# Gate and up projections with the tokens as the stationary operand, in parts of 14 and 8 column groups

## The chip, the cores and the metric

The kernel runs on one core of a Trainium2 chip. The metric is the device time of one execution in microseconds. TensorE (PE, with its weight loads as PEld), VectorE (DVE), ScalarE (ACT), GpSimd (POOL) and SyncE (SP, which issues the transfers) run side by side and wait for one another by semaphores. A matmul has a stationary operand, loaded first, and a moving one, whose columns stream through; its result lands in PSUM, which has eight banks of 512 float32 columns.

## What is computed

One layer of an encoder for 256 tokens of width 2048, conditioned by one vector c: a feed-forward, a mixer (a gated branch and latent attention side by side), a second feed-forward, and norms. Cut to what the change touches:

```
mod = silu(c) @ w_ada + b_ada                 # 9 rows of 2048: shift, scale, gate three times
n = rms(h, norm) * (1 + scale) + shift        # 256 x 2048
a = silu(n @ w_gate) * (n @ w_up)             # 256 x 5632
h = h + 0.5 * gate * (a @ w_down)             # 256 x 2048
```

All weights are float32 and are read from memory once: 2048 x 5632 for each of gate, up and down, in both feed-forwards.

## The kernel before

The activations are kept transposed, with the features on the partitions: h and n are 16 row blocks of 128 features by 256 tokens. Every matrix product is made of three: each weight block is split into a high part, rounded to the engine's fast float32 form, and a low part, the rest (`split`: one transfer into one of five raw buffers, a cast on ScalarE, line 170, and a subtraction on VectorE, line 174, for each of two halves; there are four buffers for high and four for low halves, two blocks' worth). The activations are split in the same way. High by high, high by low and low by high are added up in PSUM.

A feed-forward (`ffn`) works on 22 column groups (`pg`) of 128 x 2 gate and 128 x 2 up columns, in two halves of 11. A half first makes the products of all its groups, then its share of the down projection, so 22 slots of activations `a` (128 features x 256 tokens, high and low part, pool `actp`) are alive at a time. In `gu_chunk` a 128 x 128 weight block is stationary and the 256 tokens move:

```python
mm(o, hi[:, k, f], n[0][:, kt], first and kt == kt0 and f % 2 == 0, False)
mm(o, hi[:, k, f], n[1][:, kt], False, False)
```

so gate and up of 128 features stand side by side in one bank, features on the partitions, and `swiglu` (tanh on ScalarE, three operations on VectorE and a cast on ScalarE) turns a bank into a slot of the form that the down projection moves.

The modulation rows are made column by column: `mod_col` loads a 128 x 2048 block of w_ada (1 MB) into one of the raw buffers, and VectorE multiplies it by silu(c) and sums along the row (line 132, tile ada). There are 144 of these. Feed-forward 1 can't wait for its own: its first half goes over the 16 row blocks in groups of 3, 3, 3, 3 and 4 (`grouped`), so that each group starts when its rows are there; between groups the partial sums are copied from PSUM to SBUF (`keep_part`, line 288) and later back (`take_part`, line 292). The first three row blocks go through four column groups at once, in all eight banks. Feed-forward 2 does the same in three passes (`in_passes`). The other columns are spread over later work by lists of counts: `ADA_UP1` for the second half's up projection, `ADA_DOWN1` for the down projections and `ADA_MIX` for the mixer; `ada` pins each product behind the last subtraction of the block before it on VectorE.

The mixer's projections already hold the tokens stationary (`a_form`), 128 at a time, and move up to 512 weight columns.

The tile framework sets the order on each engine: it goes through the program with costs of its own and issues on an engine what is ready, in program order where several are. `issue_after` pins an instruction behind another one. On the chip each engine then keeps that order, waits included.

Of the kernel before, what the change touches and what calls it, by code (L numbers as in the profile page):

```python
# [2 lines left out]

# [13 lines left out]
P = 128  # L17
# [5 lines left out]
HALF_PG = 11  # L23
FK = 22
# [3 lines left out]
ADA_UP1 = (0, 2, 4, 4, 1, 1, 4, 2, 2, 2, 4)  # L28
ADA_DOWN1 = (1, 1, 1, 1, 2, 1, 0, 0, 1, 2, 2, 0, 1, 0, 1, 1)
# [3 lines left out]
    "outA": (0, 1, 1, 2, 0, 0, 0, 0), "outM": (1, 1, 0, 1, 1, 0, 0, 0),  # L33
# [37 lines left out]
def encoder_layer(ctx: ExitStack, tc: tile.TileContext, xT, pos, cst, vnorm, w_ada, gu1k, gu1, dn1,  # L71
                  win_a, win_b, wuq, wukv, w_sT, wout, gu2, dn2, outT, *gu1g):
# [50 lines left out]
    # ---- conditioning: one column of the modulation table per 128 x 2048 block of w_ada  # L123
# [38 lines left out]
    # ---- weights: exact high and low parts  # L162
# [15 lines left out]
    # ---- norms  # L178
# [6 lines left out]
    class RowNorm:  # L185
        """Root mean square over the partitions and tiles of a transposed array."""
# [57 lines left out]
    # ---- feed-forward  # L244
    def acc_of(banks, f):
        return banks[f // 2][:, (f % 2) * T : (f % 2) * T + T]

    def gu_chunk(w, banks, n, kt0, nk, first, last):
        kts = [range(kt0, kt0 + (nk + 1) // 2), range(kt0 + (nk + 1) // 2, kt0 + nk)]
        for (whi, wlo), ks in zip(w, kts):  # L250
            hi, lo = (x.rearrange("p (k f c) -> p k f c", k=len(ks), f=4) for x in (whi, wlo))
            for k, kt in enumerate(ks):
                for f in range(4):
                    o = acc_of(banks, f)
                    mm(o, hi[:, k, f], n[0][:, kt], first and kt == kt0 and f % 2 == 0, False)
                    mm(o, hi[:, k, f], n[1][:, kt], False, False)
            for k, kt in enumerate(ks):
                for f in range(4):
                    mm(acc_of(banks, f), lo[:, k, f], n[0][:, kt], False, last and kt == kt0 + nk - 1)

    def swiglu(ftmp, src, slot):
        g, u = src[:, :T], src[:, T:]
        th = ftmp.tile([P, T], F32, tag="th", name="th")
        s = ftmp.tile([P, T], F32, tag="sg", name="sg")
        a = ftmp.tile([P, T], F32, tag="a", name="a")
        act.activation(th, g, AF.Tanh, scale=0.5)
        dve.scalar_tensor_tensor(s, th, 1.0, g, op0=ALU.add, op1=ALU.mult)
        dve.tensor_tensor(a, s, u, op=ALU.mult)
        act.copy(slot[:, 0], a)  # L269
        dve.tensor_tensor(slot[:, 1], a, slot[:, 0].bitcast(F32), op=ALU.subtract)  # L270

    def ffn(gu, dn, n, gate, ada_pg, ada_dn, lead, groups, prep, norm, before_down=None):
        with tc.tile_pool(name="actp", bufs=1) as actp, tc.tile_pool(name="ftmp", bufs=2) as ftmp:
            def tag(pg):
                return "acc" if pg % 2 == 0 else "aux"

            def finish(pg, banks, slots):
                for j in range(2):
                    f = pg * 2 + j
                    slot = actp.tile([P, 2, T], F32R, tag=f"a{f % FK}", name=f"s{f}")  # L280
                    swiglu(ftmp, banks[j], slot)
                    slots.append(slot)

            def keep_part(part, pg, banks):
                for j in range(2):
                    f = pg * 2 + j
                    part[f] = actp.tile([P, 512], F32, tag=f"a{f % FK}", name=f"p{f}")
                    act.copy(part[f], banks[j])  # L288

            def take_part(part, pg, banks):  # L290
                for j in range(2):
                    act.copy(banks[j], part[pg * 2 + j])  # L292

            def in_passes(slots):
                part = {}
                for kgs in PASSES:
                    for pg in range(HALF_PG):
                        banks = [bank(tag(pg), "gu") for _ in range(2)]
                        for kg in kgs:
                            prep(kg, pg)  # L300
                            w = split(gu[pg, kg])
                            if kg and kg == kgs[0]:
                                take_part(part, pg, banks)
                            gu_chunk(w, banks, n, kg * 4, 4, kg == 0, kg == 3)
                        if kgs[-1] == 3:
                            finish(pg, banks, slots)
                        else:
                            keep_part(part, pg, banks)

            def grouped(slots):  # L310
                part = {}

                banks = [bank(tag(pg), "gu") for pg in range(4) for _ in range(2)]
                for kt in range(GROUPS[0]):
# [3 lines left out]
                    for half in range(2):  # L318
                        hi, lo = (x.rearrange("p (f c) -> p f c", f=8) for x in w[half])
                        for f in range(8):  # L320
                            o = acc_of(banks, half * 8 + f)
                            mm(o, hi[:, f], n[0][:, kt], kt == 0 and f % 2 == 0, False)
                            mm(o, hi[:, f], n[1][:, kt], False, False)
                        for f in range(8):
                            mm(acc_of(banks, half * 8 + f), lo[:, f], n[0][:, kt], False, kt == GROUPS[0] - 1)
                todo = []
# [7 lines left out]
                def load(kg, kt0, pg, a, b):  # L334
                    if a == 0:
                        prep(kg, pg)
                    return split(groups[kg][pg][:, a * 512 : b * 512], (b - a) * 512, (b - a + 1) // 2 * 512)

                w = load(*todo[0])
                for pg in range(4):  # L340
                    keep_part(part, pg, banks[2 * pg : 2 * pg + 2])
                for i, (kg, kt0, pg, a, b) in enumerate(todo):
                    if a == 0:
                        banks = [bank(tag(pg), "gu") for _ in range(2)]
                        if kg:
                            take_part(part, pg, banks)
                    gu_chunk(w, banks, n, kt0 + a, b - a, kg == 0 and a == 0, b == GROUPS[kg])
                    if i + 1 < len(todo):
                        w = load(*todo[i + 1])
                    if b == GROUPS[kg]:  # L350
                        if kg < len(GROUPS) - 1:
                            keep_part(part, pg, banks)
                        else:
                            finish(pg, banks, slots)

            for half in range(2):
                pgs = range(half * HALF_PG, half * HALF_PG + HALF_PG)
                slots = []
                if half == 0:
                    (grouped if lead is not None else in_passes)(slots)  # L360
                else:
                    for i, pg in enumerate(pgs):
                        banks = [bank(tag(pg), "gu") for _ in range(2)]
                        for kg in range(4):
                            w = split(gu[pg - (HALF_PG if lead is not None else 0), kg])
                            if kg < ada_pg[half][i]:
                                ada(1)
                            gu_chunk(w, banks, n, kg * 4, 4, kg == 0, kg == 3)
                        finish(pg, banks, slots)
                for d in range(KT):  # L370
# [3 lines left out]
                    for c2 in range(2):  # L374
                        w = split(dn[half, d, c2], 11 * P, 6 * P)
                        if c2 < ada_dn[half][d]:
                            ada(1)
# [13 lines left out]
    # ---- silu(c) * 2 on every partition  # L391
# [55 lines left out]
    # ---- feed-forward 1  # L447
# [11 lines left out]
    for kg, nk in enumerate(GROUPS[:-1]):  # L459
        at += nk  # L460
        pgs = range(4 if kg == 0 else 0, HALF_PG)
# [28 lines left out]

    ffn(gu1, dn1, n1, G1, (none, ADA_UP1), (none, ADA_DOWN1), gu1k, gu1g, prep1, norm, gate_col(G1))
# [68 lines left out]
        # low-rank queries  # L560
# [12 lines left out]
        # low-rank keys and values, shared rotary key  # L573
# [430 lines left out]
```

## Time and profile before

| | us |
|---|---|
| three runs | 1870.49, 1872.46, 1872.83 |
| median | 1872.46 |
| profiled execution: span from first to last instruction | 1868.8 |
| busy in the span: TensorE | 1834.1 |
| weight loads | 1795.9 |
| VectorE | 1324.0 |
| ScalarE | 970.1 |

The profiled execution is known by its span; what lies around the span is taken from the median of the runs, 3.7 us above it. The stages on TensorE begin at about 20 (feed-forward 1), 800 (mixer) and 1095 us (feed-forward 2).

### The profile page before, as it was taken

Reading aid. Unit: us, or ns where it says so; the run is one execution under the profiler, and the core shown is the slowest. Engines: PE = TensorE matmul, PEld = TensorE weight load, DVE = VectorE, ACT = ScalarE, POOL = GpSimd, SP = SyncE. Lnnn points to the kernel's source line nnn. Section 1 sums busy time; section 2 is a strip of 40 time slices with the busy share of each in tenths; the row PEclk is TensorE's granted clock in tenths of the full one; section 3 lists DMA queues with packets and bytes.
Section 4 is the critical chain, followed back from the end, with each engine's and each line's share of the span. In section 5 each row is a group of like instructions: output and inputs, shape, how many; then the busy total and the mean of one; then the engine's idle time right before and its main releaser. Section 6 shows DMA issues by size and latency. Waiting matters only on the chain.

```text
span 1868.8 us, 34895 instructions
## 1 busy us (share of the span) xinstructions
PE 1834.1 (98%) x14512; PEld 1795.9 (96%) x14512; DVE 1324.0 (71%) x1849; ACT 970.1 (52%) x1553; POOL 30.2 (2%) x29
## 2 busy tenths in 40 slices
PE   6999999999999999999999999999999999999997
PEld 6999999999999999988878999999999999999997
DVE  6888878776867687796877876666887655554554
ACT  3688874344444444466674554567634344443553
POOL 1000000000000000000010000000000000000000
PEclk7999999999999999999999999999999999999998
DMA  8989958997968788877855667776599755554552
GB/s 329 332 322 337 343 177 284 318 321 257 358 235 317 274 304 297 327 266 280 311 185 198 229 221 272 273 276 234 175 317 318 278 181 183 186 187 148 173 184 92
DMA packets 75326, 481.22 MB, mean 257 GB/s; under 512 B 8480, under 2 KB 9248, under 8 KB 33184
## 3 DMA queue, kind: packets, MB, share of 16 engines
q1 hardware_dynamic: 75168, 479.00, 71.7%
q8 instruction: 113, 1.85, 0.4%
q14 instruction: 45, 0.37, 0.1%
HBM read 476.87 MB, written 2.10 MB: 256 GB/s over the span
## 4 chain that ended last, share of the span: by engine, by line
PE 55%; issue 41%; DVE 2%; ACT 1%; DMA 0%; POOL 0%; DVEq 0%; SPq 0%; ACTq 0%; POOLq 0%
PE gu L121 27%; PE dn L121 14%; PE wo L121 5%; PE u L121 2%; PE v L121 2%; PE cq L121 1%; PE sc L121 1%; DVE ada L132 1%; PE ckv L121 1%; PE qproj L121 1%; PE av L121 0%; ACT whi L170 0%; DMA h<-in_xT_dram 0%; PE vproj L121 0%; PE kproj L121 0%
## 5 line engine op out<-in xcount | busy, mean ns | idle before, releaser
L174 DVE TENSOR_TENSOR wlo<-raw,whi 128x1024 fp32r<-128x1024 f32 (+3 forms) x717 | 760.7, 1067 | 425.1 <-ACT whi L170 409.2
L170 ACT CAST whi<-raw 128x1024 fp32r<-128x1024 f32 (+2 forms) x720 | 663.2, 925 | 738.4 <-PE gu L121 404.8
L121 PE MATMUL gu<-nh,whi 128*128 128x256 f32 x2816 | 695.1, 284 | 11.5 <-ACT whi L170 11.3
L121 PE MATMUL gu<-nl,whi 128*128 128x256 f32 x2816 | 694.4, 284 | 0.0
L121 PEld LDWEIGHTS gu<-nh,whi 128*128 128x128 f32 x2816 | 542.7, 193 | 12.9 <-ACT whi L170 12.5
L121 PEld LDWEIGHTS gu<-nl,whi 128*128 128x128 f32 x2816 | 542.7, 193 | 0.2 <-DVE nl L242 0.2
L121 PE MATMUL gu<-nh,wlo 128*128 128x256 f32 x2816 | 400.8, 284 | 0.0
L121 PE MATMUL dn<-s,whi 128*128 128x256 f32 x2816 | 379.6, 283 | 0.0
L121 PEld LDWEIGHTS gu<-nh,wlo 128*128 128x128 f32 x2816 | 367.1, 193 | 0.0
L121 PEld LDWEIGHTS dn<-s,whi 128*128 128x128 f32 x2816 | 356.4, 192 | 0.0
L132 DVE CUSTOM_DVE_ANT_0 ada<-ada,cb 128x2048 f32<-128x2048 f32 (+1 forms) x144 | 324.5, 2255 | 0.0
L121 PE MATMUL dn<-s,wlo 128*128 128x256 f32 x1408 | 210.7, 283 | 0.0
L121 PEld LDWEIGHTS dn<-s,wlo 128*128 128x128 f32 x1408 | 187.4, 192 | 0.0
L288 ACT COPY p<-gu 128x512 f32<-128x512 f32 x132 | 70.7, 589 | 27.3 <-PE gu L121 26.9
L292 ACT COPY gu<-p 128x512 f32<-128x512 f32 x132 | 74.3, 597 | 0.0
L387 DVE SCALAR_TENSOR_TENSOR h<-dn,mods,h 128x256 f32<-128x256 f32 x64 | 30.9, 483 | 39.4 <-PE dn L121 39.4
L241 ACT ACTIVATE nh<-nr,mods 128x256 fp32r<-128x256 f32 x48 | 23.2, 507 | 41.8 <-DVE mods L143 34.2
L121 PE MATMUL wo<-mA,whi 128*128 128x256 f32 x256 | 35.8, 288 | 0.0
L197 ACT ACTIVATE sq<-h 128x256 f32<-128x256 f32 x45 | 18.8, 418 | 30.0 <-DVE h L387 19.8
L270 DVE TENSOR_TENSOR s<-a,s 128x256 fp32r<-128x256 f32 x88 | 33.2, 418 | 0.5 <-ACT s L269 0.5
L242 DVE SCALAR_TENSOR_TENSOR nl<-nr,mods,nh 128x256 fp32r<-128x256 f32 x48 | 22.2, 481 | 15.9 <-ACT nh L241 15.8
L121 PE MATMUL wo<-mM,whi 128*128 128x256 f32 x256 | 33.3, 283 | 0.0
(206 smaller groups left out, 1045.7 us busy)
## 6 DMA issues: line engine op xcount, KB each, us to landing
ada<-in_w_ada_dram SPq DMA_DIRECT2D x144, 1024.0 KB, 6.6
raw<-in_gu_dram SPq DMA_DIRECT2D x143, 1024.0 KB, 5.1
raw<-in_dn_dram SPq DMA_DIRECT2D x128, 704.0 KB, 5.3
raw<-in_gu_dram SPq DMA_DIRECT2D x40, 768.0 KB, 6.2
raw<-in_win_a_dram SPq DMA_DIRECT2D x20, 1024.0 KB, 6.6
raw<-in_wout_dram SPq DMA_DIRECT2D x16, 1024.0 KB, 5.1
raw<-in_gu1k_dram SPq DMA_DIRECT2D x3, 1024.0 KB, 8.8
raw<-in_wuq_dram SPq DMA_DIRECT2D x4, 768.0 KB, 5.0
```

The source lines that it names most:

```text
L121: return pe.matmul(out, w, x, start=start, stop=stop, skip_group_check=True)
L132: dve.tensor_tensor_reduce(out=w[:, sl], in0=w[:, sl], in1=cb[:, sl], scale=0.5, scalar=acc if i else 0.0, op0=ALU.mult, op1=ALU.add, accu ...
L170: mark["act"] = act.copy(hi, raw[:, a:b])
L174: mark["dve"] = dve.tensor_tensor(lo, raw[:, a:b], hi.bitcast(F32), op=ALU.subtract)
L197: act.activation(sq, src, AF.Square)
L241: act.activation(hi, nr, AF.Identity, bias=s)
L242: dve.scalar_tensor_tensor(lo, nr, s, hi.bitcast(F32), op0=ALU.add, op1=ALU.subtract)
L270: dve.tensor_tensor(slot[:, 1], a, slot[:, 0].bitcast(F32), op=ALU.subtract)
L288: act.copy(part[f], banks[j])
L292: act.copy(banks[j], part[pg * 2 + j])
L387: dve.scalar_tensor_tensor(h[:, d], o, mods[:, gate, d : d + 1], h[:, d], op0=ALU.mult, op1=ALU.add)
```

## The change

Gate and up now take 128 tokens as the stationary operand and move 512 columns: for each row block of a column group, two gate and two up blocks side by side, once for each half of the tokens. The products come out with tokens on the partitions. `finish` makes the swiglu in that form, and a `flip`, queued behind the matmuls of the next step, transposes the group's 256 features by four matmuls with the identity into a PSUM bank, from which ScalarE casts the high part and VectorE subtracts the low part of two slots at once. The halves become parts of 14 and 8 groups (`FIRST`), and with them the down projections: two blocks of 14 slots for each output row block in the first, one of 16 in the second. `run` holds a common loop for all steps; it puts the partial sums of the next step into its banks right behind the matmuls of this one, before this step's sums are kept. The counts in the `ADA` lists are new. The weights are laid out to match on the host. Comments were dropped.

```diff
-HALF_PG = 11
-FK = 22
+FIRST = 14
 GROUPS = (3, 3, 3, 3, 4)
 PASSES = ((0, 1), (2,), (3,))
 EARLY = 4 * len(PASSES[0])
-ADA_UP1 = (0, 2, 4, 4, 1, 1, 4, 2, 2, 2, 4)
-ADA_DOWN1 = (1, 1, 1, 1, 2, 1, 0, 0, 1, 2, 2, 0, 1, 0, 1, 1)
+ADA_UP1 = (2, 3, 2, 3, 2, 3, 2, 3)
+ADA_DOWN1 = ((0, 0, 0, 1) * 4, (1, 1, 1, 1, 1, 1, 1, 1, 1, 1, 1, 1, 1, 1, 0, 0))
 ADA_MIX = {
     "ckv": (2, 1, 0, 1), "v0": (0, 1, 0, 1), "v1": (1, 0, 0, 0),
     "u0": (1, 2, 0, 2), "u1": (1, 1, 1, 0),
-    "outA": (0, 1, 1, 2, 0, 0, 0, 0), "outM": (1, 1, 0, 1, 1, 0, 0, 0),
+    "outA": (0, 1, 1, 2, 0, 0, 0, 0), "outM": (1, 1, 1, 1, 1, 1, 1, 0),
 }
...
             for k, kt in enumerate(ks):
-                for f in range(4):
-                    o = acc_of(banks, f)
-                    mm(o, hi[:, k, f], n[0][:, kt], first and kt == kt0 and f % 2 == 0, False)
-                    mm(o, hi[:, k, f], n[1][:, kt], False, False)
+                for t in range(2):
+                    mm(banks[t], n[0][:, kt, token(t)], hi[:, k], first and kt == kt0, False)
+                    mm(banks[t], n[1][:, kt, token(t)], hi[:, k], False, False)
             for k, kt in enumerate(ks):
-                for f in range(4):
-                    mm(acc_of(banks, f), lo[:, k, f], n[0][:, kt], False, last and kt == kt0 + nk - 1)
-
-    def swiglu(ftmp, src, slot):
+                for t in range(2):
+                    mark["gu"] = mm(banks[t], n[0][:, kt, token(t)], lo[:, k], False, last and kt == kt0 + nk - 1)
...
-        act.copy(slot[:, 0], a)
-        dve.tensor_tensor(slot[:, 1], a, slot[:, 0].bitcast(F32), op=ALU.subtract)
+        return a
...
+            flips = []
+
             def finish(pg, banks, slots):
-                for j in range(2):
-                    f = pg * 2 + j
-                    slot = actp.tile([P, 2, T], F32R, tag=f"a{f % FK}", name=f"s{f}")
-                    swiglu(ftmp, banks[j], slot)
-                    slots.append(slot)
+
+                a = [swiglu(ftmp, banks[t]) for t in range(2)]
+                slot = actp.tile([P, 2, 2, T], F32R, tag=f"a{pg % FIRST}", name=f"s{pg}")
+                slots += [(slot[:, 0, j], slot[:, 1, j]) for j in range(2)]
+
+                def flip():
+                    ps = bank(tag(pg), "tps")
+                    with tc.issue_after(mark["gu"].ins):
+                        for j in range(2):
+                            for t in range(2):
+                                o = j * T + t * P
+                                pe.matmul(ps[:, o : o + P], a[t][:, j * P : j * P + P], ident, start=o == 0, stop=True,
+                                          is_transpose=True, skip_group_check=True)
+                    hi, lo = (slot[:, i].rearrange("p a b -> p (a b)") for i in range(2))
+                    act.copy(hi, ps)
+                    dve.tensor_tensor(lo, ps, hi.bitcast(F32), op=ALU.subtract)
+
+                flips.append(flip)
+
+            def turn(n=1):
+                for _ in range(min(n, len(flips))):
+                    flips.pop(0)()
...
             def take_part(part, pg, banks):
-                for j in range(2):
-                    act.copy(banks[j], part[pg * 2 + j])
+                for t in range(2):
+                    act.copy(banks[t], part[pg][:, t])
+
+            def run(steps, part, slots):
+
+
+                def begin(pg, kt0, nk, opens, load, more):
+                    w = load()
+                    if not opens:
+                        return w, banks
+                    new = [bank(tag(pg), "gu") for _ in range(2)]
+                    if kt0:
+                        take_part(part, pg, new)
+                    return w, new
+
+                banks = None
+                w, banks = begin(*steps[0])
+                for i, (pg, kt0, nk, opens, load, more) in enumerate(steps):
+                    gu_chunk(w, banks, n, kt0, nk, kt0 == 0, kt0 + nk == KT)
+                    if not opens or nk == 4:
+                        turn()
+                    old = banks
+                    if i + 1 < len(steps):
+                        w, banks = begin(*steps[i + 1])
+                    if kt0 + nk == KT:
+                        finish(pg, old, slots)
+                    elif not more:
+                        keep_part(part, pg, old)
...
-                    for pg in range(0 if kg else 4, HALF_PG):
-                        todo += [(kg, kt0, pg, a, b) for a, b in zip(cuts, cuts[1:])]
+                    for pg in range(0 if kg else 4, FIRST):
+                        steps += [(pg, kt0 + a, b - a, a == 0, partial(load, kg, pg, a, b), b < nk)
+                                  for a, b in zip(cuts, cuts[1:])]
...
+            def rest(slots):
+                def load(pg, kg):
+                    w = split(gu[pg - (FIRST if lead is not None else 0), kg])
+                    if kg < ada_pg[pg - FIRST]:
+                        ada(1)
+                    return w
+
+                run([(pg, kg * 4, 4, kg == 0, partial(load, pg, kg), kg < 3)
+                     for pg in range(FIRST, NPG) for kg in range(4)], {}, slots)
...
+                chunks, size = ((2, FIRST), (1, 2 * (NPG - FIRST)))[half]
+                cut = (size + 1) // 2
                 for d in range(KT):
                     if half == 0 and before_down:
                         before_down(d)
                     o = bank("acc" if d % 2 else "aux", "dn")[:, :T]
-                    for c2 in range(2):
-                        w = split(dn[half, d, c2], 11 * P, 6 * P)
-                        if c2 < ada_dn[half][d]:
-                            ada(1)
-                        for part_, k0 in ((0, 0), (1, 6)):
+                    for c2 in range(chunks):
+                        w = split(dn[half][d, c2], size * P, cut * P)
+                        if not c2:
+                            ada(ada_dn[half][d])
+                        for part_, (k0, k1) in enumerate(((0, cut), (cut, size))):
                             hi, lo = (x.rearrange("p (k c) -> p k c", c=P) for x in w[part_])
-                            ks = range(6 if part_ == 0 else 5)
-                            for k in ks:
-                                a = slots[c2 * 11 + k0 + k]
-                                mm(o, hi[:, k], a[:, 0], c2 == 0 and part_ == 0 and k == 0, False)
-                                mm(o, hi[:, k], a[:, 1], False, False)
-                            for k in ks:
-                                mm(o, lo[:, k], slots[c2 * 11 + k0 + k][:, 0], False, c2 == 1 and k0 + k == 10)
+                            if part_:
+                                turn()
+                            for k in range(k0, k1):
+                                a = slots[c2 * size + k]
+                                mm(o, hi[:, k - k0], a[0], c2 == 0 and k == 0, False)
+                                mm(o, hi[:, k - k0], a[1], False, False)
+                            for k in range(k0, k1):
+                                mark["gu"] = mm(o, lo[:, k - k0], slots[c2 * size + k][0], False,
+                                                c2 == chunks - 1 and k == size - 1)
                     dve.scalar_tensor_tensor(h[:, d], o, mods[:, gate, d : d + 1], h[:, d], op0=ALU.mult, op1=ALU.add)
```

## Rows read from the trace of the kernel before

**Rows 1.** The page: busy time by engine, and granted clock over 40 slices.

```profile
span 1868.8 us, 34895 instructions
...
PE 1834.1 (98%) x14512; PEld 1795.9 (96%) x14512; DVE 1324.0 (71%) x1849; ACT 970.1 (52%) x1553; POOL 30.2 (2%) x29
...
PEclk7999999999999999999999999999999999999998
```

**Rows 2.** The chain of waits: start us, us, engine, tile, line, count.

```profile
42.27 28.88 PE gu L121 x226
...
72.76 4.35 PE gu L121 x34
...
79.11 210.50 PE gu L121 x1752
289.61 126.72 PE dn L121 x1056
416.33 253.44 PE gu L121 x2112
...
822.87 14.07 PE ckv L121 x96
836.94 0.87 PE tp L540 x8
...
849.40 21.77 PE v L121 x96
...
972.55 0.44 PE tpp L806 x4
...
993.02 0.59 PE tpp L806 x4
```

**Rows 3.** The page: groups, with busy us, mean ns, idle before.

```profile
L121 PE MATMUL gu<-nh,whi 128*128 128x256 f32 x2816 | 695.1, 284 | 11.5 <-ACT whi L170 11.3
...
L292 ACT COPY gu<-p 128x512 f32<-128x512 f32 x132 | 74.3, 597 | 0.0
```

**Rows 4.** Windows: stretch, its us, busy by engine (instructions), clock, DMA share, GB/s.

```profile
120.00:160.00 40.00, 40.00 (x336) 40.00 (x335) 31.70 (x42) 34.67 (x60) 0.00 (x0) 1.00 0.89 320
...
669.80:796.50 126.70, 126.70 (x1059) 126.70 (x1057) 99.12 (x128) 57.78 (x83) 0.00 (x0) 1.00 0.86 306
416.30:669.80 253.50, 253.50 (x2115) 253.50 (x2114) 184.16 (x205) 103.69 (x130) 0.00 (x0) 1.00 0.81 291
740.00:760.00 20.00, 20.00 (x169) 20.00 (x168) 18.12 (x25) 8.98 (x13) 0.00 (x0) 1.00 0.95 373
1052.00:1070.00 18.00, 18.00 (x152) 18.00 (x151) 17.94 (x30) 9.34 (x14) 0.00 (x0) 1.00 0.98 362
```

**Rows 5.** VectorE in order of time, from 290 us.

```profile
291.12 0.74 DVE L268 TENSOR_TENSOR a<-sg,gu 128x256 f32<-128x256 f32 x2
```

**Rows 6.** VectorE's groups by form.

```profile
L174 DVE TENSOR_TENSOR wlo<-raw,whi 128x1024 fp32r<-128x1024 f32 x405 | 495.0, 1226 | 309.5 <-ACT whi L170 308.7 <-PE u L121 0.4
L132 DVE CUSTOM_DVE_ANT_0 ada<-ada,cb 128x2048 f32<-128x2048 f32 x136 | 314.8, 2316 | 0.0
...
L201 DVE TENSOR_TENSOR acc<-acc,sq 128x256 f32<-128x256 f32 x48 | 20.1, 418 | 1.8 <-ACT sq L197 1.8
...
L646 DVE TENSOR_TENSOR kn<-kproj,stats 128x512 f32<-128x512 f32 x4 | 2.6, 686 | 3.5 <-POOL stats L182 3.5
```

**Rows 7.** ScalarE's groups by form.

```profile
L170 ACT CAST whi<-raw 128x1024 fp32r<-128x1024 f32 x408 | 427.7, 1050 | 441.3 <-PE gu L121 374.0 <-PE wo L121 23.8 <-PE v L121 13.1
...
L266 ACT ACTIVATE th<-gu 128x256 f32<-128x256 f32 x88 | 28.7, 379 | 0.2
...
L807 ACT COPY pp<-tpp 128x512 f32<-128x512 f32 x8 | 4.7, 586 | 6.9 <-PE tpp L806 6.9
```

**Rows 8.** VectorE in order of time, w_out's second half.

```profile
1059.54 0.48 DVE L826 SCALAR_TENSOR_TENSOR h<-wo,mods,h 128x256 f32<-128x256 f32 x1
...
1065.62 0.47 DVE L826 SCALAR_TENSOR_TENSOR h<-wo,mods,h 128x256 f32<-128x256 f32 x1
```

More of the change, by code (lines that the diff above doesn't have):

```diff
@@ L2 @@
 from contextlib import ExitStack
+from functools import partial
 import concourse.bass as bass
@@ L242, in make_n, with token @@
         dve.scalar_tensor_tensor(lo, nr, s, hi.bitcast(F32), op0=ALU.add, op1=ALU.subtract)
-    def acc_of(banks, f):
-        return banks[f // 2][:, (f % 2) * T : (f % 2) * T + T]
+    def token(t):
+        return slice(t * P, t * P + P)
     def gu_chunk(w, banks, n, kt0, nk, first, last):
@@ L290, in take_part @@
             def take_part(part, pg, banks):
-                for j in range(2):
-                    act.copy(banks[j], part[pg * 2 + j])
-            def in_passes(slots):
[L295 to L308, printed above, removed]
+                for t in range(2):
+                    act.copy(banks[t], part[pg][:, t])
@@ L310, in grouped @@
+            def in_passes(slots):
+                def load(pg, kg):
+                    prep(kg, pg)
+                    return split(gu[pg, kg])
+                run([(pg, kg * 4, 4, kg == kgs[0], partial(load, pg, kg), kg != kgs[-1])
+                     for kgs in PASSES for pg in range(FIRST) for kg in kgs], {}, slots)
             def grouped(slots):
@@ L318, in grouped, with load @@
                     for half in range(2):
[L319 to L326, printed above, removed]
+                        hi, lo = (x.rearrange("p (f c) -> p f c", f=2) for x in w[half])
+                        for f in range(2):
+                            for t in range(2):
+                                o = banks[half * 4 + f * 2 + t]
+                                mm(o, n[0][:, kt, token(t)], hi[:, f], kt == 0, False)
+                                mm(o, n[1][:, kt, token(t)], hi[:, f], False, False)
+                        for f in range(2):
+                            for t in range(2):
+                                mm(banks[half * 4 + f * 2 + t], n[0][:, kt, token(t)], lo[:, f], False, False)
+                def load(kg, pg, a, b):
+                    if a == 0:
+                        prep(kg, pg)
+                    w = split(groups[kg][pg][:, a * 512 : b * 512], (b - a) * 512, (b - a + 1) // 2 * 512)
+                    if kg == 0 and pg == 4:
+                        for q in range(4):
+                            keep_part(part, q, banks[2 * q : 2 * q + 2])
+                    return w
+                steps = []
                 kt0 = 0
@@ L339, in grouped @@
[L339 to L354, printed above, removed]
+                run(steps, part, slots)
@@ L358, in ffn @@
                 slots = []
-                if half == 0:
+                if half:
+                    rest(slots)
+                else:
                     (grouped if lead is not None else in_passes)(slots)
[L361 to L366, printed above, removed]
-                                ada(1)
-                            gu_chunk(w, banks, n, kg * 4, 4, kg == 0, kg == 3)
-                        finish(pg, banks, slots)
+                chunks, size = ((2, FIRST), (1, 2 * (NPG - FIRST)))[half]
@@ L460, in encoder_layer @@
         at += nk
-        pgs = range(4 if kg == 0 else 0, HALF_PG)
+        pgs = range(4 if kg == 0 else 0, FIRST)
         jobs = [(m, d) for d in range(at, at + GROUPS[kg + 1]) for m in (SC1, SH1)]
@@ L489, in encoder_layer @@
     norm = RowNorm(KT)
-    ffn(gu1, dn1, n1, G1, (none, ADA_UP1), (none, ADA_DOWN1), gu1k, gu1g, prep1, norm, gate_col(G1))
+    ffn(gu1, (dn1a, dn1b), n1, G1, ADA_UP1, ADA_DOWN1, gu1k, [gu1g[f"gu1_{g}"] for g in range(len(GROUPS))], prep1, norm, gate_col(G1))
     rb2 = norm.done(ones_d, True)
@@ L881, in encoder_layer @@
     cut = EARLY // 4
[L882 removed]
+    steps = [(kg, pg) for kgs in PASSES[:-1] for pg in range(FIRST) for kg in kgs][cut:]
     jobs = [(m, d) for d in range(EARLY, KT) for m in (SC3, SH3)]
[L884 to L885 removed]
+    for i, at in enumerate(steps):
+        ahead3[at] = jobs[i * len(jobs) // len(steps) : (i + 1) * len(jobs) // len(steps)]
     def prep3(kg, pg):
@@ L900, in encoder_layer @@
     norm = RowNorm(KT)
-    ffn(gu2, dn2, n3, G3, (none, none), (none, none), None, None, prep3, norm, gate_col(G3))
+    ffn(gu2, (dn2a, dn2b), n3, G3, none, (none, none), None, None, prep3, norm, gate_col(G3))
     rb = norm.done(ones_d)
@@ L971, in _layout @@
         "gu1k": gu1k,
-        "gu1": keep(gu1[HALF_PG:]),
-        "dn1": down(a["ffn1_w_down"][0]),
+        "gu1": keep(gu1[FIRST:]),
+        **down("dn1", a["ffn1_w_down"][0]),
         "win_a": keep(win_a),
```

45 lines of the change are left out of this document (20 added, 25 removed).

## The prediction

> **What bounds the kernel now.** I read the page's busy shares first: TensorE is busy 98% of the span at a granted clock of 0.9 and more of full in nearly every slice, VectorE 71%, ScalarE 52% [rows 1]. A busy TensorE need not be an efficient one, so I went on to the chain of waits, which gives stretches with their number of matmuls. From 79.11 to 796 us it is four unbroken stretches on TensorE, and nothing else [rows 2] (the fourth, the second down stretch, is as long as the first one). In the second gate and up stretch 2,112 matmuls take 253.44 us, 120.0 ns each; in each down stretch 1,056 take 126.7, again 120.0. So TensorE sets the time, and what sets its pace is the interval between matmuls (the 284 ns that the groups give for one is its length in the pipeline [rows 3], not its share of time). In the windows, ScalarE is busy 34.67 of 40 us while partial sums are kept and put back, and VectorE with the DMA engines is close to full in two short stretches [rows 4]: these come next when TensorE gets faster.
>
> **The change, part by part.**
>
> *Tokens stationary.* The weights were the stationary operand and 256 token columns moved; now 128 tokens stand and 512 weight columns move, so 2,816 x 3 = 8,448 matmuls [rows 3] become 4,224. This form is in the trace already: the mixer's v projection does 96 such matmuls in 21.77 us, 226.8 ns each, and the 320-column form does 96 in 14.07, 146.6 each [rows 2]. The three sizes lie on one line: (226.8 - 120.0) / 256 = 0.417 ns per column and 13.2 ns per matmul (320 columns: 133.5 + 13.2 = 146.7). So a pair of old matmuls, 240.0, becomes one of 226.8, and 13.2 ns go. Of the 4,224 pairs the first two lead-in row blocks (48 pairs) lie before 42 us, where TensorE waits for others; 4,176 x 13.2 = **-55.1 us**. The operands and their order are those of the mixer rows, so I take no other price; the bounds are 0 and 56.
>
> The Trainium skill ("TensorE: Matmul & The Clock Gate", Back-to-back issue gap) gives a warm matmul its columns / 2.4 plus 2.5 ns. By that a pair saves 2.5 ns, 10.4 us in all, and the change would lose. The trace disagrees: 120.0 ns for 256 columns where the page's formula has 109.2.
>
> *Transposes.* The product now comes out with tokens on the partitions, so each of 22 column groups in both feed-forwards needs four 128 x 128 float32 transposes. The mixer's rows show eight in 0.87 us and four in 0.44, with 0.59 for four at worst [rows 2]. 44 x 0.44 = **+19.4 us** (19.1 at the rate of the eight; 26.0 at the worst row). They stand one step (5.4 us) behind the gate and up matmuls that feed them. Where the chain before them can be seen, at 289.61, VectorE ends the last product at 291.86, 2.3 us behind TensorE's last matmul [rows 2, 5]; so TensorE doesn't wait for them in the middle of a half. Without that cover 44 x 2.3 = 101 us would show.
>
> *The end of a half.* There the cover is the first part of the down weights: 7 slots x 3 x 0.12 = 2.5 us in the first half, 8 slots = 2.9 in the second, against 2.3. Just enough, but VectorE may have a modulation product (2.3 us [rows 6]) in between, and in the second half the slots just transposed are wanted 1.4 us later, while cast and subtraction take 0.59 [rows 7] and 0.69 [rows 6]. 0.5 us for each of four ends: **+2** (0 to 8).
>
> *Lead-in.* Between 42 and 79 us TensorE idles twice, 71.15 to 72.76 and 77.11 to 79.11 [rows 2], 3.6 us, because the modulation of row blocks 3 to 5 is late. The first group of three now has ten steps instead of seven ahead of those blocks: 3 x 18 x 0.2268 = 12.2 us more of matmuls that are due anyway, against 3 x 0.786 MB, 6.5 us at the 362 GB/s of the fullest window [rows 4]. The waits go: **-3** (0 to -3.6).
>
> *Partial sums.* With 14 groups in the first half, 112 copies out and 112 back in feed-forward 1 and 56 and 56 in feed-forward 2, 168 of each instead of 132 [rows 3]: 36 x (0.586 + 0.597) = 42.6 us more of ScalarE (the copy out by the row of the same form [rows 7]). Putting them back a step ahead gains nothing by itself: in the stretch from 79 us TensorE already runs at 210.50 / 1,752 = 120.15 ns, so no put-back is waited for. But the cover is thinner. ScalarE's work is 34.67 x 4.32 / 40 = 3.74 us per three-block step (36 x 0.12 = 4.32 us of TensorE), and the new step is 18 x 0.2268 = 4.08: 92% full for 42 steps. In feed-forward 2's third pass a step is 5.44 us, with two casts of weights (2.1), two copies back (1.2), two tanh (0.8) and a cast (0.6) [rows 3, 7]: 86%. Two steps of split weights lie ready, so I take **+1** (0 to 8, an estimate: one copy of 0.60 late on a quarter of 56 steps).
>
> *Modulation columns, moved.* Feed-forward 1's second up part has 20 instead of 26, its first down projection four where it had none, its second down 14 as before but in 16 rows of 16 slots instead of 22, and w_out's second half 7 instead of 4. The first two have room (291 GB/s and less than three quarters of VectorE in the up part now [rows 4]); the last two have little. In the second down projection a row takes 48 x 0.12 = 5.76 us of TensorE. It asks 2 x 1,024 KB of the DMA engines, 364 GB/s, where the window at 1052 shows 362 at a share of 0.98 and that at 740 shows 373 at 0.95 [rows 4]; and of VectorE two subtractions, a product, the row's update and the norm's sum, 2 x 1.226 + 2.316 + 0.48 + 0.418 = 5.7 us [rows 6, 8]. Both just fit: **+2** (0 to 10; at 350 GB/s, the 306 / 0.86 of this stage with room for smaller blocks, a row takes 5.99, 14 x 0.23 = 3.2). Behind a waiting product on VectorE stand the next subtraction and, through it, TensorE. In w_out, a pair with a product took VectorE 6.08 us, 1059.54 to 1065.62 [rows 8], against 5.76 of TensorE: seven in a row lag 2.2 us, within the two steps of split weights and given back in the last pair. **+1** (0 to 6).
>
> *At nothing.* The down matmuls stay 4,224, in fewer and larger blocks (less per-instruction time on ScalarE, which has room there). The swiglu's last subtraction is half as many instructions of twice the size. On SP the weight and modulation transfers keep their order within a step; only free raw buffers, still five, hold them. If that cover went, it would show in the two tight stretches above.
>
> **Sum.** -55.1 + 19.4 + 2 - 3 + 1 + 2 + 1 = -32.7 on a span of 1868.8, so 1836.1. The median of the runs is 1872.46, 3.7 above that span, for what lies around it; the time is 1872.5 - 32.7 = **1839.8**. All bounds in its favour give -55.1 + 19.1 - 3.6 = -39.6, 1833; all against, without the lead-in's gain, -55.1 + 26.0 + 8 + 8 + 10 + 6 = +2.9, 1875.
>
> **Rivals.**
> - The tight stretches bind. ScalarE at 92%, VectorE at 5.7 of 5.76 and the DMA engines at 364 GB/s leave no room, and waits of half their upper bounds or more come in: +8 to +20, 1848 to 1860. For it: the 17.94 of 18 us of VectorE at 1052. Against: TensorE didn't wait in that very window [rows 4].
> - Partial sums come back late (slower). ScalarE, in order, waits for TensorE's last matmul to keep a step's sums, and the next put-back stands behind it. Then each of 84 steps (56 in feed-forward 1, 28 in feed-forward 2) waits up to 1.19 us, 100 us in all, 1940; it decides from 32.7 / 84 = 0.39 us per step. Against: ScalarE gets ahead by its split buffers today at 87%.
> - The 13.2 ns stay (slower). If the fixed part belongs to what is written and not to the instruction, pairing saves next to nothing: 1872.5 + 19.4 + 3 = 1895. It decides under 19.4 / 4,176 = 4.6 ns per pair. Against: three sizes on one line. With the 2.5 ns of the Trainium skill's page above it is 1884.5.
> - The gain is hidden anyway: something else holds the span. Against: four stretches without a gap.
>
> **How the numbers follow.** The forecast, 1833 to 1848, has 0.65; tight stretches, up to 1860, 0.23; late partial sums 0.05; the 13.2 ns staying 0.02; no change within 0.2% (3.7 us, about what a measurement can tell) 0.03; under 1833, 0.02. Predicted is 1840. The range 1831 to 1858 leaves out the top of the tight case and the slow ones, about 2 in 10. Faster: 0.65 + 0.23 + 0.02 = 0.90; same 0.03; slower 0.07.
>
> **What would show it.** Gate and up intervals of 226.8 ns with no gap in the middle of a stretch; 176 transposes at 0.11 us; the second gate and up stretch of feed-forward 1 at 8 x 4 x 24 x 0.2268 = 174.2 us plus seven groups' transposes, 3.1; no idle TensorE from 50 us on; the second down stretch at 92.2 us and one group's transposes, and each microsecond above that is the tight stretch's. The prediction is wrong if the interval is above 232, if TensorE waits for "gu<-p" copies in the groups, or if the second down stretch goes beyond 102.

## The result, and the profile after

The changed kernel takes 1846.71 us (median; runs 1845.79 to 1847.06) against 1871.93 for the kernel before on the same chip: a ratio of 0.9866, with a 95% interval of 0.9852 to 0.988. That is 25.2 us; 32.7 were forecast (from 1872.46, the median of the three runs known then), to 1840, in a range of 1831 to 1858. The profiled span went from 1868.8 to 1844.0 us, by 24.8.

The page of the changed kernel, its busy time by engine and its granted clock [rows 1]:

```profile
span 1844.0 us, 26484 instructions
...
PE 1804.7 (98%) x10464; PEld 1591.7 (86%) x10464; DVE 1317.6 (71%) x1753; ACT 989.7 (54%) x1523; POOL 31.2 (2%) x29
...
PEclk8999999999999999999999999999999999999998
```

TensorE still sets the time, at the same clock, with 4,048 matmuls fewer (4,224 less 176 transposes). Weight loads, which were nearly as busy as the matmuls (96% and 98%), have fallen to 86%. The chain of waits of the changed kernel (start us, us, what) shows both what was gained and what is missing [rows 2]:

```profile
41.12 229.66 PE gu L121 x1004
270.80 1.05 ACT whi L170
271.86 0.49 ACT gu L309
272.39 4.84 PE gu L121 x20
277.26 1.05 ACT whi L170
278.31 0.49 ACT gu L309
278.85 4.84 PE gu L121 x20
...
538.29 0.44 PE tps L290 x4
538.72 21.80 PE gu L121 x96
...
688.52 2.87 PE dn L121 x24
691.95 89.16 PE dn L121 x743
```

In feed-forward 1's second part 96 matmuls of 512 columns take 21.80 us, 227.1 ns each (226.8 expected), and four transposes 0.44. From 41 to 270 us nothing interrupts the matmuls: 229.66 us for 1,004, where 1,004 x 0.2268 = 227.7; most of the rest stands before 80 us, where the granted clock is 0.96. But from 270.8 on a new pattern repeats every 6.46 us: 20 matmuls, a weight cast on ScalarE, a copy of partial sums back into PSUM (gu<-p, line 309), 20 matmuls. This is feed-forward 1's last group of row blocks, whose steps should take 24 x 0.2268 + 0.44 = 5.88 us. ScalarE in order of time in one such step:

```profile
296.62 1.05 ACT L170 CAST whi<-raw 128x1024 fp32r<-128x1024 f32 x1 [1.44 <-PE gu L121]
297.58 0.58 ACT L309 COPY gu<-p 128x512 f32<-128x512 f32 x1
298.10 0.58 ACT L293 CAST s<-tps 128x512 fp32r<-128x512 f32 x1
298.58 0.59 ACT L309 COPY gu<-p 128x512 f32<-128x512 f32 x1
299.10 0.66 ACT L266 ACTIVATE th<-gu 128x256 f32<-128x256 f32 x2
300.58 1.05 ACT L170 CAST whi<-raw 128x1024 fp32r<-128x1024 f32 x1 [0.83 <-PE gu L121]
303.08 1.05 ACT L170 CAST whi<-raw 128x1024 fp32r<-128x1024 f32 x1 [1.44 <-PE gu L121]
```

The reader is to see that ScalarE is idle for 1.44 and 0.83 us of each step and yet puts the next step's sums back only at 297.58, right behind a weight cast, when TensorE is at its transposes and out of other work. TensorE in order of time at the same place:

```profile
297.34 0.60 PE L290 MATMUL tps<-cs,a 128*128 128x128 f32 x4
298.21 0.50 PE L121 MATMUL gu<-whi,nh 128*128 128x512 f32 x1 [0.28 <-ACT gu L309]
298.55 0.40 PE L121 MATMUL gu<-whi,nl 128*128 128x512 f32 x1
```

Groups and waits after, beside [rows 3]:

```profile
L121 PE MATMUL gu<-whi,nh 128*128 128x512 f32 x1408 | 554.9, 395 | 14.9 <-ACT whi L170 8.6 <-ACT gu L309 6.1
```

Counted by this row the put-backs cost 6.1 us in all; the steps say 0.58 each. Twelve steps in each feed-forward have transposes ahead of a put-back, 24 in all (the expectations below count 25), which makes 13.9 us. A row of waits begins at the modelled end of the instruction before. Here that is the last of four transposes, at 297.94, while four in a stream take 0.44 us of TensorE, up to 297.78; and the first matmul behind the wait takes 0.34 us to the start of the next instead of 0.23. So 0.28 + 0.16 + 0.11 = 0.55 of the 0.58 us can be found in the rows. Start to start is the measure.

The stages account for the difference. Feed-forward 1, from the third lead-in block to the end of its last down matmul, fell from 754.2 us (42.27 to 796.49) to 740.0 (41.12 to 781.11); feed-forward 2, from one norm's power on GpSimd to the next, from 764.4 to 753.9; the mixer grew from 292.9 to 294.0; the lead-in ends 1.15 us earlier; the rest is as before: -14.2 - 10.5 + 1.1 - 1.15 = -24.8.

### The profile page after: what moved, and what is told of

It reads as the page before. It is cut to its first block, busy times and chain, and to the rows that moved or that the text cites. A ratio compares the mean times of both kernels' runs of the same rounds, so it can differ in the third digit from the quotient of the medians.

```text
span 1844.0 us, 26484 instructions
## 1 busy us (share of the span) xinstructions
PE 1804.7 (98%) x10464; PEld 1591.7 (86%) x10464; DVE 1317.6 (71%) x1753; ACT 989.7 (54%) x1523; POOL 31.2 (2%) x29
## 4 chain that ended last, share of the span: by engine, by line
PE 54%; issue 41%; DVE 2%; ACT 2%; POOL 0%; DMA 0%; DVEq 0%; SPq 0%; ACTq 0%; POOLq 0%
PE gu L121 25%; PE dn L121 14%; PE wo L121 5%; PE u L121 2%; PE v L121 2%; PE cq L121 1%; PE sc L121 1%; DVE ada L132 1%; ACT whi L170 1%; PE ckv L121 1%; PE qproj L121 1%; PE av L121 0%; DVE wlo L174 0%; ACT gu L309 0%; PE vproj L121 0%
## 5 line engine op out<-in xcount | busy, mean ns | idle before, releaser
L170 ACT CAST whi<-raw 128x1024 fp32r<-128x1024 f32 (+3 forms) x662 | 653.2, 993 | 704.8 <-PE gu L121 357.1
L174 DVE TENSOR_TENSOR wlo<-raw,whi 128x1024 fp32r<-128x1024 f32 (+4 forms) x659 | 751.2, 1149 | 372.3 <-ACT whi L170 367.4
L121 PE MATMUL gu<-whi,nh 128*128 128x512 f32 x1408 | 554.9, 395 | 14.9 <-ACT whi L170 8.6
L121 PE MATMUL gu<-whi,nl 128*128 128x512 f32 x1408 | 551.2, 392 | 0.0
L121 PE MATMUL gu<-wlo,nh 128*128 128x512 f32 x1408 | 386.5, 391 | 0.0
L121 PEld LDWEIGHTS gu<-whi,nh 128*128 128x128 f32 x1408 | 265.7, 189 | 75.8 <-ACT gu L309 11.9
L121 PEld LDWEIGHTS gu<-wlo,nh 128*128 128x128 f32 x1408 | 266.0, 189 | 55.9 <-DVE wlo L174 0.3
L121 PEld LDWEIGHTS gu<-whi,nl 128*128 128x128 f32 x1408 | 266.1, 189 | 54.0
L121 PEld LDWEIGHTS dn<-s,wlo 128*128 128x128 f32 x1408 | 182.8, 192 | 0.0
L305 ACT COPY p<-gu 128x512 f32<-128x512 f32 x168 | 89.7, 589 | 14.7 <-PE gu L121 14.5
L267 DVE SCALAR_TENSOR_TENSOR sg<-th,gu 128x256 f32<-128x256 f32 x88 | 33.2, 416 | 0.0
L268 DVE TENSOR_TENSOR a<-sg,gu 128x256 f32<-128x256 f32 x88 | 33.0, 415 | 0.0
```

The lines of the kernel that those rows point to most:

```text
L121: return pe.matmul(out, w, x, start=start, stop=stop, skip_group_check=True)
L170: mark["act"] = act.copy(hi, raw[:, a:b])
L174: mark["dve"] = dve.tensor_tensor(lo, raw[:, a:b], hi.bitcast(F32), op=ALU.subtract)
L305: act.copy(part[pg][:, t], banks[t])
```

## The experiments

The runs come from three chips, on which the kernel before took 1870.87 us (the first four runs below), 1872.07 (the two with halves of 11 that follow, and the last one on w_out) and 1871.57 us (tokens stationary alone, and the parts alone), beside 1871.93 with the result; a difference between runs of different chips can be off by about a microsecond.

Three theories of the 6.46 us steps were set against each other. **Theory 1:** order in PSUM. Each of the two PSUM tags has four banks. In the program the transposes of a group (`turn`) come ahead of `begin` of the next step, and both take banks of the same tag (`tag(pg)`, the next group but one has the same parity). The banks are handed out in program order, so the put-back can only be issued once the transposes have theirs, and these are pinned behind the step's last matmul. **Theory 2:** ScalarE has too much to do in these steps. **Theory 3:** the put-back stands on ScalarE behind a weight cast that waits for a free split buffer.

**The transposes' bank from the other tag.**

```diff
-                    ps = bank(tag(pg), "tps")
+                    ps = bank(tag(pg + 1), "tps")
```

> Only the bank of the transposes is taken from the other of the two PSUM tags (bank(tag(pg + 1))). Theory 1, the transposes' bank stands ahead of the next put-back's banks in one ring, so the put-back can't be issued before the transposes, which stand behind the step's last matmul: the put-back moves a step ahead, the 25 last-pass steps of 6.45 us become 5.88 (5.44 + 0.44), and the time falls by 25 x 0.57 = 14.2 us to 1832.5 (1830 to 1835). Theory 2, ScalarE has too much to do in these steps: it stays busy as much, steps stay at 6.3 to 6.5 us and the time at 1845 to 1848. Theory 3, the put-back stands behind a weight cast that waits for a free split buffer: no buffer was added, so 1843 to 1848.

Measured: 1833.66 us, ratio 0.9801 (0.9786 to 0.9816). 13 us come back through one bank's name.

**The next step begun before the transposes.**

```diff
-                    if not opens or nk == 4:
-                        turn()
                     old = banks
                     if i + 1 < len(steps):
                         w, banks = begin(*steps[i + 1])
+                    if not opens or nk == 4:
+                        turn()
```

> The transposes' bank stays in the same tag, but the next step is begun (its banks taken, its sums put back) before the transposes of the group before are queued. Theory 1: the same 14.2 us as with the other bank, 1831 to 1836, last-pass steps of 5.88 us. Theories 2 and 3: 1843 to 1848, steps of 6.3 to 6.5 us.

Measured: 1832.16 us, ratio 0.9795 (0.978 to 0.9809), 14.5 less than the change. ScalarE in order of time in the same steps:

```profile
294.29 1.05 ACT L170 CAST whi<-raw 128x1024 fp32r<-128x1024 f32 x1 [1.42 <-PE gu L121]
295.25 0.64 ACT L266 ACTIVATE th<-gu 128x256 f32<-128x256 f32 x2
295.79 0.59 ACT L293 CAST s<-tps 128x512 fp32r<-128x512 f32 x1
296.25 0.61 ACT L309 COPY gu<-p 128x512 f32<-128x512 f32 x1
297.24 0.59 ACT L309 COPY gu<-p 128x512 f32<-128x512 f32 x1 [0.37 <-DVE s L294]
297.76 1.05 ACT L170 CAST whi<-raw 128x1024 fp32r<-128x1024 f32 x1
300.20 1.05 ACT L170 CAST whi<-raw 128x1024 fp32r<-128x1024 f32 x1 [1.39 <-PE gu L121]
```

The same instructions, as many, in another order: the copies still follow the transposes' cast, but now they belong to the step after the one that TensorE is about to start. A step takes 5.91 us. ScalarE had time: theory 2 falls. Theory 3 names what the copy stood behind, but not why: the weight cast waits as long for its buffer here (1.42 and 1.39 us), and no buffer was added; in the changed kernel the copy for the very next step came behind it, and the order in which the banks are taken decided that.

**No transposes.** The kernel leaves them out; the slots are cast straight from the products:

```diff
-                    ps = bank(tag(pg), "tps")
-                    with tc.issue_after(mark["gu"].ins):
...
-                    act.copy(hi, ps)
-                    dve.tensor_tensor(lo, ps, hi.bitcast(F32), op=ALU.subtract)
+                    for j in range(2):
+                        act.copy(slot[:, 0, j], a[j])
+                        dve.tensor_tensor(slot[:, 1, j], a[j], slot[:, 0, j].bitcast(F32), op=ALU.subtract)
```

> Leaves out the transposes: the slots are cast straight from the products with tokens on the partitions (as many elements as before, the output is not the reference's). Theory 1: both the 44 x 0.44 = 19.4 us of transposes and the 14.2 us of waits go, 1846.7 - 33.6 = 1813 (1810 to 1817), last-pass steps of 5.44 us. Theory 3: the put-back still stands behind the cast, which was 1.5 us behind the buffer; without the transposes to cover it the wait grows from 0.57 to about 1.0 per step, so only 19.4 less 11 go, 1835 to 1840. Theory 2: ScalarE's work per step stays 4.5 us of 5.44, 1825 to 1830.

Measured: 1811.56 us, ratio 0.9684 (0.9668 to 0.97). Against the run with the put-back first the transposes cost 1832.2 - 1811.6 = 20.6 us, 0.47 for each of 44 groups (0.44 by the rows). The waits went with them, as theory 1 has it (its expectation held).

**The put-back late, as in the kernel before.** The third part of the change undone:

```diff
-                    new = [bank(tag(pg), "gu") for _ in range(2)]
-                    if kt0:
-                        take_part(part, pg, new)
-                    return w, new
+                    return w, [bank(tag(pg), "gu") for _ in range(2)]
...
                         keep_part(part, pg, old)
+                    if i + 1 < len(steps) and steps[i + 1][3] and steps[i + 1][1]:
+                        take_part(part, steps[i + 1][0], banks)
```

> Undoes the third part of the change: the next step's sums are put back after this step's are kept or its products made, as in the kernel before. In the grouped steps and the second pass nothing is expected of it (the kernel before ran them at 120.15 ns per matmul that way). In the last pass, by theory 1, the put-back now stands behind the transposes and their cast on ScalarE (0.5 us) too: steps of 6.9 to 7.1 us and 25 x 0.5 = 12 us more, 1857 to 1862. If the place of the put-back in the program means nothing, 1845 to 1848.

Measured: 1869.87 us, ratio 0.9993 (0.9983 to 1.0002): slower than the change by 23, twice what was expected, and no faster than the kernel before. The row of TensorE's waits for the put-back (us in total, how many, the longest), and then ScalarE and TensorE in order of time at one step:

```profile
PE gu L121 <- ACT gu L309: 30.3, 24, 1.3
```

```profile
308.58 1.05 ACT L170 CAST whi<-raw 128x1024 fp32r<-128x1024 f32 x1 [1.67 <-PE gu L121]
309.54 0.65 ACT L266 ACTIVATE th<-gu 128x256 f32<-128x256 f32 x2
310.08 0.58 ACT L293 CAST s<-tps 128x512 fp32r<-128x512 f32 x1
310.54 1.13 ACT L309 COPY gu<-p 128x512 f32<-128x512 f32 x2
```

```profile
309.29 0.60 PE L290 MATMUL tps<-cs,a 128*128 128x128 f32 x4
311.21 0.50 PE L121 MATMUL gu<-whi,nh 128*128 128x512 f32 x1 [1.31 <-ACT gu L309]
```

The copies for the very next step stand behind the tanh and the transposes' cast; a step is 7.5 us, 1.0 more than in the change. I had counted the cast alone (0.5), and the time lies outside what was expected.

**Halves of 11.** The parts of 14 and 8 undone, with the old modulation counts:

```diff
-FIRST = 14
+FIRST = 11
...
-                chunks, size = ((2, FIRST), (1, 2 * (NPG - FIRST)))[half]
+                chunks, size = 2, FIRST
```

> Undoes the parts of 14 and 8 alone: halves of 11, the down projections in two blocks of 11 slots and the modulation counts of the kernel before; tokens stay stationary and the put-back stays a step ahead. Theory 1 (the parts only move waits): the first group of three has 7 steps again, so 3 to 5 us of idle TensorE come back before 80 us; the last passes have about 19 waiting steps of 0.57 us instead of 25 (-3.4) and w_out's second half ends as before (-1.1): 1843 to 1849 in all. Rival (the parts are needed to feed the faster steps): more than 8 us slower than the change, 1855 or more.

Measured: 1857.86 us, ratio 0.9924 (0.9908 to 0.9941), 11.2 slower than the change. This expectation failed, and the rival held. The 11.2 are what is left of a larger loss: with 11 groups six waiting steps fewer (18 x 0.58 instead of 24 x 0.58, 3.5 us) and w_out's 1.1 us are in this run's favour.

**Halves of 11, the next step begun first.** Both edits together.

> Halves of 11 as in the run before this one, and the next step begun before the transposes are queued. Theory 1: the waits of the last passes go here too, so 1832.2 + 3.6 to 5 for the lead-in - 1.1 for w_out = 1834 to 1837. Rival: 1840 or more.

Measured: 1848.02 us, ratio 0.9873 (0.9858 to 0.9888), 15.9 slower than the same with 14 and 8; the rival held here too. The windows of this kernel (stretch, us, busy PE, PEld, DVE, ACT, POOL, clock, DMA share, GB/s), and then of the one with 14 and 8:

```profile
41.00:80.00 39.00, 34.94 (x142) 27.70 (x141) 32.73 (x43) 26.01 (x45) 2.46 (x1) 0.94 0.88 323
80.00:340.00 260.00, 254.05 (x1307) 217.12 (x1306) 206.55 (x294) 186.16 (x310) 0.00 (x0) 0.98 0.82 289
```

```profile
41.00:80.00 39.00, 39.00 (x166) 32.07 (x167) 33.09 (x42) 26.35 (x43) 2.46 (x1) 0.96 0.89 319
80.00:340.00 260.00, 260.00 (x1170) 215.06 (x1169) 200.66 (x278) 216.56 (x368) 0.00 (x0) 1.00 0.80 284
```

With halves of 11 TensorE is idle for 4.1 and 6.0 us more in these two stretches, and its granted clock is 0.94 and 0.98 instead of 0.96 and 1.00, which costs about another 39 x 0.02 = 0.8 and 260 x 0.02 = 5.2 us of full-speed time (the clock is rounded to hundredths, so by 1.3 us more or less): 16 together. By the marks used above, feed-forward 1 takes 750.3 us instead of 733.9, the mixer 1.1 less, and feed-forward 2 746.6 in both. So the loss is in feed-forward 1's first part, where the modulation counts that this edit also changes have not begun.

The idle times end at 66.1, 77.1, 182.8, 202.9 and 221.8 us, all in the first and the fourth group of row blocks. At four of the five the chain goes on ScalarE from the copy of kept sums through the making of a normalised row block of the next group (nh, line 241), which needs its modulation columns, to the weight cast that TensorE waits for; at 202.9 it goes through the copies and the cast alone. What three row blocks take of TensorE is now 11 x 18 x 0.2268 = 44.9 us instead of 47.5; 14 groups give 57.2. An estimate from the sizes of the transfers: a step of 4.08 us brings 0.786 MB of weights, and a share of the next group's columns, 1.049 MB each. With 11 groups the first group's seven steps have six columns and the fourth's eleven have eight, 413 and 380 GB/s; the other two ask 333. With 14 no group asks more than 347. The idle times are where the demand is highest. VectorE's products grow with the same columns, and which of the two is late was not tried.

**Tokens stationary alone.** Halves of 11 and the late put-back, the edits of two runs above together.

> Tokens stationary alone: halves of 11, the old modulation counts, and the next step's sums put back after this step's are kept, as before. If the three parts' costs add up: 1857.9 with halves of 11, and on each of about 19 last-pass steps the 0.9 us more that the late put-back cost per step with parts of 14 and 8 (23.2 us on 25 steps), 1875 (1872 to 1879): the new form alone is slower than the kernel before. If the late put-back matters only together with the parts of 14: 1856 to 1860.

Measured: 1875.84 us, ratio 1.0019 (1.0009 to 1.0028). The costs do add up as expected (18 steps wait for the put-back here): the new form by itself loses 4 us.

**Parts of 14 and 8 alone**, in the kernel before, with its weights stationary:

```diff
-HALF_PG = 11
-FK = 22
+FIRST = 14
+FK = 2 * FIRST
...
-                pgs = range(half * HALF_PG, half * HALF_PG + HALF_PG)
+                pgs = range(FIRST, NPG) if half else range(FIRST)
```

> Parts of 14 and 8 and the new modulation counts alone: weights stationary, 256 tokens moving, put-back as in the kernel before. If the parts only give the first groups more matmuls to stand before the modulation columns that they wait for: the 3.6 us of idle TensorE before 80 us go, about 1 comes back in w_out, 1868 to 1871. If the 36 more copies out and back or the modulation columns in the 16-slot down projection cost time by themselves: 1874 or more.

Measured: 1870.34 us, ratio 0.999 (0.998 to 1.0). In its window from 41 to 80 us TensorE is busy 38.40 of 39.00 where it was 34.57; as expected, and about all it gives.

**w_out's second half with 4 modulation columns**, on top of the put-back first:

```diff
-ADA_UP1 = (2, 3, 2, 3, 2, 3, 2, 3)
+ADA_UP1 = (3, 3, 2, 3, 3, 3, 3, 3)
...
-    "outA": (0, 1, 1, 2, 0, 0, 0, 0), "outM": (1, 1, 1, 1, 1, 1, 1, 0),
+    "outA": (0, 1, 1, 2, 0, 0, 0, 0), "outM": (1, 1, 0, 1, 1, 0, 0, 0),
```

> Parts of 14 and 8, the next step begun before the transposes, and w_out's second half back at 4 modulation columns (1, 1, 0, 1, 1, 0, 0, 0), the other three moved into feed-forward 1's second up part (3, 3, 2, 3, 3, 3, 3, 3). If VectorE's lag in w_out (6.08 us of work per pair against 5.76) is what ends the mixer 1.1 us later: 1831 (1830 to 1832), and the mixer from its first projection to the third norm takes 292.9 us instead of 294. If that 1.1 us is something else: 1832 to 1834.

Measured: 1831.46 us, ratio 0.978 (0.9765 to 0.9794). The third norm's power on GpSimd, in this run and in the changed kernel:

```profile
1072.02 0.70 POOL L225 TENSOR_TENSOR stats<-stats,half_m 128x2 f32<-128x2 f32 x1 [59.21 <-DVE stats L223]
```

```profile
1077.73 1.62 POOL L225 TENSOR_TENSOR stats<-stats,half_m 128x2 f32<-128x2 f32 x1 [59.45 <-DVE stats L223]
```

From the first projection (779.88 here, 785.37 there) to its end the mixer takes 292.8 us against 294.0: the 1.1 us are w_out's. Of those, 0.9 are the instruction itself, 1.62 instead of 0.70 us on GpSimd, so VectorE's lag, which the expectation had named, costs only 0.2. In the changed kernel VectorE runs a subtraction beside that instruction (from 1077.58 to 1078.81), in this run nothing; whether that makes it longer was not tried. In the whole time the gain over 1832.16 lies within the runs' spread. This is the fastest version here, 40.6 us under the kernel before.

## Why the prediction was right, and where it was off

- *Tokens stationary, -55.1.* Right. The mixer's 226.8 ns carried over: 227.1 in the new stage. By the formula of the Trainium skill ("TensorE: Matmul & The Clock Gate", Back-to-back issue gap), which the page gives for an isolated warm matmul, these would be 215.8; the trace disagrees on 512 columns as it did on 256. At the 2.5 ns of that page of the Trainium skill for each of 4,224 matmuls saved, the new form would give 10.6 us, an estimate, less than the 20.6 of the transposes; the trace's pairs went from 240.0 to 227.1 ns, which on 4,176 pairs is 53.9 us.
- *Transposes, +19.4.* Right: 20.6 by the run without them. They are not waited for in the middle of a part.
- *The ends of the parts, +2.* Too much: at 688.52 the 24 matmuls of 2.87 us are followed by the rest 0.56 later, 0.44 of it the transposes. About 0.1 each.
- *Lead-in, -3.* Right for the change (no idle TensorE from 41 to 270 us, and the 3.6 us are gone; 3.8 less idle in the run with the parts alone). But it was too small a part of what the 14 groups do. I priced them against the old pace. At the new pace halves of 11 cost 11 us (or 16 with the put-back first), in the fourth group as well as in the first.
- *Partial sums, +1.* This is the step that failed. It measured 13.9 by the steps, and 13.0 and 14.5 came back in the two runs that change the order, outside the 0 to 8 given. By a sign that the prediction set itself, TensorE waiting for "gu<-p" copies, it is wrong here, though the total lies in its range. The rival named the place and the price that decides (0.39 us per step), and took all 84 steps; it came in 24, those with transposes ahead of a put-back, at 0.58. I had argued from ScalarE's load, 86 to 92%, which was no problem: the grouped steps run without a gap, and the last ones wait with ScalarE idle for 2.3 of 6.46 us. What I missed is the order: the transposes and the put-back share the banks of a tag, and in the program the transposes come first. I had also written that putting back a step ahead gains nothing by itself. No wait for a put-back shows in the rows of the kernel before (120.15 ns per matmul there), and a put-back ahead was not tried in it; for this one the statement is wrong: without it the time is 1869.9.
- *The tight stretches.* The second down projection was given +2 (with 14 columns "as before"; the old counts in the diff make 15) and ran 92.7 us from 688.5 (92.2 and one group's transposes were foreseen), at 336 GB/s and a DMA share of 0.91; w_out was given +1 and took 1.1, though 0.9 of it by the longer instruction on GpSimd and not by VectorE's lag:

```profile
688.50:781.20 92.70, 92.70 (x777) 92.70 (x775) 79.30 (x94) 41.08 (x51) 0.00 (x0) 1.00 0.91 336
```

```profile
1035.00:1055.00 20.00, 20.00 (x169) 20.00 (x169) 19.93 (x34) 9.11 (x14) 0.00 (x0) 1.00 0.98 356
```

VectorE with no free time at all (19.93 of 20) did not stop TensorE, as in [rows 4]; it only ended late.

With the terms as the rows after show them, -53.9 + 19.4 + 13.9 - 3.6 + 1.1 and the 1.15 us of an earlier lead-in give -24.3, and the span fell by 24.8. That the total came out near was luck in part: 12.9 us too little for the put-backs were met by about 4 set aside for the second down projection and the ends, which were not needed, and by 1.75 more from the lead-in. Shown by runs: the price of the transposes, the order of put-back and transposes, the need for the 14 groups, w_out. Only read from traces: the saving per matmul, and that with 11 groups the steps wait for the making of the next group's row blocks.

## What to carry to other kernels

In this framework a new user of a pool (here the transposes' bank) stands in the order in which the pool is handed out, and everything that takes from the pool after it inherits its place in time; ask of each such allocation what the instruction behind it is pinned to, before asking whether an engine has time. When the bounding engine gets faster, re-price the covers at the new pace: a part that gives 1 us to the old kernel (14 and 8 groups) gave 11 to 16 to the new one, and one part alone made it slower. A wait repeated every step is measured start to start of the step, not by the wait's row.

## What was not expected of the hardware

The rows that name TensorE's waits show 6.1 us for all the put-backs of the changed kernel where each of 24 steps loses 0.58 us, for the reason given above. And TensorE's clock bears idle times differently: 0.28 us every 6.46 us left the granted clock at 1.00 throughout the last group. With halves of 11 and the put-back first, after 1.79 us of idle time up to 66.11 the clock was granted 1.00 from 66 to 76, and after 1.88 us up to 202.93 it was 1.00 from 204 to 212. After 2.27 us up to 77.08 it was 0.50 from 79 to 81, that is, 1.2 GHz, and after another 1.79 us, up to 182.79, 0.57 from 184 to 186. So the length of one idle time does not tell what the clock will do; what does was not tried.
